# Transformer block on one core: the D weights of the up stage at another place in SBUF, and their passes in another order

## The chip, the core and the metric

The kernel runs on one core of a Trainium2 chip. The time is the device time of one execution in microseconds (us); three runs of the kernel before took 632.88, 635.07 and 636.14 us, so the median is 635.07 us. The core has five engines, each with an instruction stream of its own: TensorE (PE; its weight loads are listed apart, as PEld), VectorE (DVE), ScalarE (ACT), GpSimd (POOL) and SyncE (SP). Data lie in SBUF, in 128 partitions; an address here is a byte offset within a partition, the same for all partitions. TensorE sums into PSUM banks of 512 float32 per partition.

## The reference, cut to what matters

One transformer block over 512 tokens of width 1024. Around the change it is the feed-forward part:

```python
h = rmsnorm(x, mlp_pre_g)
gu = h @ w_gate_up                      # 1024 -> 2 * 2816
a, u = jnp.split(gu, [D_FF], axis=-1)
a = causal_dwconv(a, conv_w, conv_b)    # three taps along the tokens
y = (jax.nn.gelu(a, approximate=True) * u) @ w_down
x = x + rmsnorm(y, mlp_post_g)
```

Attention (compressed, selected, windowed) comes ahead of it, and a gated addition behind it. All in float32.

## The kernel before, in words

Every large product is done with split operands. A float32 matrix is cut into a high half (rounded to float32r, by ScalarE) and a low half (the rest, by VectorE: raw minus high). A product of weights w and activations x is then three passes of TensorE, w_high x_high + w_low x_high + w_high x_low, all summed into one PSUM tile. `mm3` (line 513) issues these three, in this order. One pass is one weight load of 128 x 128 and one matmul that streams 256 or 512 columns.

The up stage (`mlp_up`) makes the 22 pairs of 128 columns of "a" and "u". The first five pairs are done plainly. The other 17 ("blocked") use a scheme with seven half-size products in place of eight: `blocked_ops` (line 1743) writes, for each, the products named 1 to 7, each with four weight tiles of 128 x 128 times 256 columns, so 4 x 3 = 12 passes; 84 passes a block. Products 1 and 2 use the weights called A, 3 and 6 use X, 5 and 7 use Y, and product 4 uses D. X and its like are sums of loaded weights, made by VectorE. A, X and Y are 1024 wide and their halves live in two tiles each of tag "wh" (six tiles); D is 512 wide, and both its halves share one tile of tag "wd" (one tile, 1024 elements): high half in front, low half behind (`split_ops`, line 1639).

The activations of products 4, 5, 6 and 7 are sums of the normed input over token halves, made once by `half_ops` (line 1849) and split into tiles of 2 x 512 elements, high then low. Their tags are listed in `PTAG`. Product 4 uses the entries 1, 3, 5 and 7 of that list: one tile in "pt", one in "tt", one in "p", one in "kn".

The order of work: the up stage writes each operation with an engine, an estimated duration, its dependencies and a due time; `order` plays them through a small model, and the instructions are issued in the order that comes out. `products_in_order` fixes TensorE's own order: 2, 6, 7, 5, then product 1 of the next block, then 3 and 4. So product 4 is followed by product 2 of the next block. Product 4 is entered with a dependency on the low half of D. Each engine then runs its instructions strictly in that order, and waits at the first one whose input isn't there.

Where tiles lie: SBUF tiles of one pool are laid out by tag in the order in which the tags first appear, each tag taking the number of its tiles times the widest of them. The "u" tiles start at 5824, which is 192 modulo 512, and are 4096 bytes long, so all of them, with "pt" (from 182976) and "tt", are at 192 modulo 512. Tiles of "p" and "kn" are 1088 and 1216 elements wide (4352 and 4864 bytes, an odd multiple of 256), so they alternate between 192 and 448; the "kn" tile that product 4 reads is at 139200, which is 448. Behind "kn" stands a gap of 48 elements (192 bytes, `GAPS["wh"]`), which is made when the first "wh" tile is made (line 117, `real`), then the "wd" tile at 153984, then the six "wh" tiles from 158080. Both are at 384 modulo 512, so all weights of the up stage lie 192 bytes off the activations modulo 512, the low half of D too, since it starts 2048 bytes behind the high one.

Of the kernel before, what the change touches and what calls it, by code (L numbers as in the profile page):

```python
# [11 lines left out]
F32 = mybir.dt.float32  # L12
F32R = mybir.dt.float32r
# [4 lines left out]
P = 128  # L18
T = 512
D = 1024  # L20
# [21 lines left out]


SLOTS = {"u": 25, "kn": 4, "p": 6, "pt": 3, "tt": 2, "wh": 6, "wd": 1}
GAPS = {"wh": 48, "pt": 80}
P_WIDTH, KN_WIDTH = 1088, 1216


YTAG = ["u"] * 17 + ["kn"] * 3 + ["p"] * 2
# [38 lines left out]
PTAG = ["pt", "pt", "pt", "tt", "tt", "p", "p", "kn"]  # L88
# [16 lines left out]
class Tile:  # L105
# [11 lines left out]
    def real(self):  # L117
        if self.tile is None:
            pool, tag = self.rec.pools[self.pool], self.kw.get("tag")
            if self.pool == "up" and tag in self.rec.gaps:  # L120
                pool.tile([P, self.rec.gaps.pop(tag)], F32, tag="before_" + tag, name="before_" + tag, bufs=1)
                if tag == "wh":
                    pool.tile([P, D], F32R, tag="wd", name="wd", bufs=1)
            self.tile = pool.tile(list(self.shape), self.dtype, **self.kw)
        return self.tile

# [70 lines left out]
class Engine:  # L197
# [3 lines left out]
    def __getattr__(self, name):  # L201
        f = getattr(self.engine, name)
        if name == "to_reg":
            return f

        def call(*a, **k):
            if self.rec.on:
                return self.rec.add(self.name, name, a, k)
            return f(*map(real, a), **{m: real(x) for m, x in k.items()})  # L209

        return call
# [16 lines left out]
class Recorder:  # L228
    ENGINES = dict(tensor="PE", scalar="ACT", vector="DVE", gpsimd="POOL", sync="SP")

    def __init__(self, nc, pools):
        self.pools, self.nodes, self.on, self.over = pools, [], False, False
        self.strict, self.before = False, {}
        self.gaps = dict(GAPS)
        for e in self.ENGINES:
# [196 lines left out]
class Block:  # L432
# [1153 lines left out]
    def op(self, key, engine, us, run, deps=(), due=0.0, ready=0.0, takes=(), frees=()):  # L1586

        self.ops[key] = dict(engine=engine, us=us, run=run, deps=deps, due=due, ready=ready, takes=takes, frees=frees)
        return key
# [49 lines left out]
    def split_ops(self, key, src, n, due, deps, tag="wh", ready=-99.0, frees=(), low_deps=()):  # L1639

        nc, w = self.nc, self.w

        def high():
            if tag == "wh":
                w[key] = [self.up.tile([P, n], F32R, tag=tag, name=self.nm("wh"), bufs=SLOTS[tag]) for _ in range(2)]
            else:
                t = self.u([P, 2 * n], F32R, tag)
                w[key] = [t[:, i * n : (i + 1) * n] for i in range(2)]
            return [nc.scalar.activation(w[key][0], src(), AF.Copy)]

        def low():
            return [nc.vector.tensor_sub(w[key][1], src(), w[key][0].bitcast(F32))]

        if tag == "wh":
            deps, self.turn = deps + self.turn, ((key, "hi"),)
        self.op((key, "hi"), "ACT", HIGH_US if n == D else ACT_US, high, deps, due - 1.6, ready, takes=(tag,))
        self.op((key, "lo"), "DVE", LOW_US if n == D else TT_US, low, ((key, "hi"),) + low_deps, due, frees=frees)
# [85 lines left out]
    def blocked_ops(self, j, t, cyc):  # L1743

        nc, w = self.nc, self.w
# [3 lines left out]
        ht = self.ht  # L1749
        op = lambda i: (lambda k: ht[2 * k + i // 2][:, :, HALF[i % 2]])  # L1750
# [4 lines left out]
        n = BLOCKED.index(j)  # L1755
        fresh = n < len(ETAGS)
        etag = "ps" + ETAGS[n] if fresh else "e"
        tag = next(cyc)
# [35 lines left out]
        def product(ps, wt, first, op, begins=False, ends=False, wide=False):  # L1794
            def run():
                if wide and fresh:
                    self.banks.append(self.ps(ETAGS[n]))
                if ps == "h" and begins:
                    v["h"] = self.ps(tag)
                o = dict(h=lambda: v["h"][:, a], p=lambda: e()[:, a], q=lambda: e()[:, b])[ps]()  # L1800
                for k in range(4):
                    x = op(k)
                    if wide and fresh and k == 0:
                        hi, lo = (m[:, first * P : (first + 1) * P] for m in w[j, wt])
                        mm = functools.partial(nc.tensor.matmul, skip_group_check=True)
                        self.held(mm(e(), hi, x[:, None, 0, :].broadcast_to([P, 2, H]), start=True, stop=False))
                        mm(o, lo, x[:, 0, :], start=False, stop=False)
                        mm(o, hi, x[:, 1, :], start=False, stop=False)
                    else:
                        self.mm3(o, w[j, wt], (first + k) * P, x, begins and k == 0, ends and k == 3, keep=k == 0, shared=True)  # L1810
            return run
# [37 lines left out]
    def half_ops(self, due):  # L1849

        nc, fs, ht, ts = self.nc, self.f2, self.ht, []

        def sums(p, i):
            f = fs[p]
            b = lambda r, h: f[:, r, HALF[h]]
            if i == 0:
                ts.append(self.u([P, 4, H]))
            t = ts[p]
            if i == 0:
                q = f.rearrange("p r (h n) -> p (r h) n", h=2)  # L1860
                return [nc.vector.tensor_sub(t[:, 0:3:2, :], q[:, 0:4:3, :], b(0, 1)[:, None, :].broadcast_to([P, 2, H]))]
            if i == 1:
                return [nc.vector.scalar_tensor_tensor(t[:, 1, :], t[:, 0, :], -1.0, b(1, 1), op0=ALU.mult, op1=ALU.subtract)]
            return [nc.vector.scalar_tensor_tensor(t[:, 3, :], t[:, 1, :], -1.0, b(1, 0), op0=ALU.mult, op1=ALU.subtract)]

        part = lambda p, i: ts[p][:, 2 * i : 2 * i + 2, :].rearrange("p a n -> p (a n)")

        def high(p, i):
            ht.append(self.u([P, 2, T], F32R, PTAG[2 * p + i]))
            return [nc.scalar.activation(ht[2 * p + i][:, 0, :], part(p, i), AF.Copy)]  # L1870

        def low(p, i):
            o = ht[2 * p + i]
            return [nc.vector.tensor_sub(o[:, 1, :], part(p, i), o[:, 0, :].bitcast(F32))]

        prev = ()
        for p in range(KC // 2):
            t = due - 3.6 * (KC // 2 - 1 - p)
            for i in range(3):
                prev = self.op(("ht", p, i), "DVE", SUM_US if i else TT_US, functools.partial(sums, p, i), prev and (prev,), t - 3.5)  # L1880
            for i in range(2):
                prev = self.op(("ht", p, f"hi{i}"), "ACT", ACT_US, functools.partial(high, p, i), (prev,), t - 2)
                self.op(("ht", p, f"lo{i}"), "DVE", TT_US, functools.partial(low, p, i), (prev,), t)
# [286 lines left out]
```

## Time and profile before

| what | value |
|---|---|
| median of three runs | 635.07 us |
| profiled execution | 635.09 us, of which the span is 633.4 us |
| TensorE busy | 627.0 us (99% of the span), 4037 matmuls |
| VectorE busy | 513.4 us (81%) |
| ScalarE busy | 397.9 us (63%) |
| GpSimd busy | 156.5 us (25%) |
| up stage's blocked part | about 296 to 466 us of the span |

How to read it: the profile comes from one execution, so its rows are summed against 635.09 us. A row of a group names the line of the source (L209 is a helper's line that most of the second half of the kernel shares), the engine, the operation, the tile written and the tiles read (numbers left out), the shape and the count. "mlpup", "mlpdown", "norm" and "plegate" are stages, in this order; "psmm", "pss", "pst" and "pso" are PSUM tiles by their tag. A matmul of the up stage that reads "mlpup_u,mlpup_u" belongs to product 4, as D's weights are in a tile that is named like the activations. Durations of matmuls are modelled and overlap, so the time from one pass to the next is taken from their starts.

### The profile page before, as it was taken

What the parts mean: (1) busy time and instruction counts of PE and PEld (TensorE: products, weight loads), DVE (VectorE), ACT (ScalarE), POOL (GpSimd) and SP (SyncE); (2) the same over time, 40 slices, a digit from 0 to 9 for tenths busy, and PEclk for the clock granted to TensorE, in tenths of its full rate; (3) what the DMA queues carried; (4) which work ended last, traced back from release to release, by engine and by line L of the source; (5) the groups of instructions that cost most, each with busy time, mean ns of one, the idle gap of its engine ahead of it and who ended that gap; (6) DMA issues with size and microseconds to landing.
All of it is one profiled execution on the core that took longest, in us unless ns stands there. A gap on an engine that the chain in (4) does not pass through costs nothing.

```text
span 633.4 us, 11279 instructions
## 1 busy us (share of the span) xinstructions
PE 627.0 (99%) x4037; PEld 568.5 (90%) x4037; DVE 513.4 (81%) x1038; ACT 397.9 (63%) x773; POOL 156.5 (25%) x239
## 2 busy tenths in 40 slices
PE   9999999999999999999999999999999999999997
PEld 8988888888888887888999999999988999999986
DVE  6696679988967579699899999999998985856973
ACT  7546589889998568474676676766754543343251
POOL 2011397778686000211001100102100010201000
PEclk9999999999999999999999999999999999999999
DMA  8516922311321757485467576677844534367032
GB/s 296 172 76 213 230 79 67 84 45 40 77 74 52 283 203 294 161 206 116 121 197 182 169 164 182 162 209 212 218 129 126 156 95 122 116 252 266 2 116 84
DMA packets 45576, 95.79 MB, mean 151 GB/s; under 512 B 4560, under 2 KB 14160, under 8 KB 45264
## 3 DMA queue, kind: packets, MB, share of 16 engines
q1 hardware_dynamic: 40496, 84.57, 40.2%
q0 software_dynamic: 4880, 10.49, 9.9%
q8 instruction: 32, 0.52, 0.3%
q14 instruction: 24, 0.20, 0.1%
q10 hardware_dynamic: 144, 0.00, 0.0%
HBM read 81.42 MB, written 9.44 MB: 143 GB/s over the span
## 4 chain that ended last, share of the span: by engine, by line
PE 92%; DVE 6%; issue 1%; ACT 1%; ACTq 0%
PE mlpup_psmm L209 21%; PE fill_psmm L428 10%; PE mlpdown_pst L209 6%; PE mlpup_pss L209 6%; PE mlpdown_pss L209 5%; PE mlpdown_psmm L209 4%; PE nsa_pss L428 3%; DVE mlpup_u L209 3%; PE nsa_pso L428 3%; PE mlpup_pst L209 3%; PE norm_pss L209 3%; PE nsa_pst L428 3%; PE projq_psmm L428 3%; PE vnatural_pss L428 2%; PE projk_psmm L428 2%; PE compress_psmm L428 2%
## 5 line engine op out<-in xcount | busy, mean ns | idle before, releaser
L209 PE MATMUL mlpup_psmm<-r_u,mlpup_wh 128*128 128x256 f32 (+1 forms) x612 | 77.9, 280 | 0.0
L209 PEld LDWEIGHTS mlpup_psmm<-r_u,mlpup_wh 128*128 128x128 f32 x612 | 74.7, 188 | 0.3
L209 PE MATMUL mlpup_psmm<-mlpup_u,mlpup_wh 128*128 128x256 f32 (+1 forms) x474 | 69.1, 295 | 0.5 <-DVE mlpup_wh L209 0.5
L209 PEld LDWEIGHTS mlpup_psmm<-mlpup_u,mlpup_wh 128*128 128x128 f32 x474 | 62.6, 188 | 3.5 <-DVE mlpup_wh L209 0.9
L209 POOL DMA_DIRECT2D mlpup_u<-in_gs_dram x17 | 20.9, 1230 | 153.6 <-DVE mlpup_s L209 54.9
L209 ACT ACTIVATE mlpup_wh<-mlpup_u 128x1024 fp32r<-128x1024 f32 x37 | 39.2, 1061 | 17.6 <-PE mlpup_psmm L209 13.9
L209 ACT ACTIVATE mlpdown_wh<-mlpdown_wr 128x1024 fp32r<-128x1024 f32 (+1 forms) x24 | 23.7, 988 | 37.4 <-PE mlpdown_pst L209 8.8
L209 DVE TENSOR_TENSOR mlpup_wh<-mlpup_u,mlpup_wh 128x1024 fp32r<-128x1024 f32 x37 | 45.2, 1221 | 0.4 <-ACT mlpup_wh L209 0.3
L428 PE MATMUL fill_psmm<-loadx_u,fill_wh 128*128 128x512 f32 x144 | 45.0, 401 | 0.0
L209 PE MATMUL mlpdown_pst<-mlpup_u,mlpdown_wh 128*128 128x512 f32 (+1 forms) x228 | 44.6, 338 | 0.0
L209 PEld LDWEIGHTS mlpdown_pst<-mlpup_u,mlpdown_wh 128*128 128x128 f32 x228 | 36.8, 188 | 4.8
L428 POOL TENSOR_SCALAR nsa_u<-nsa_u,nsa_nrc,vnatural_u 128x512 f32<-128x512 f32 (+3 forms) x64 | 38.2, 610 | 8.3 <-DVE nsa_nrc L428 6.4
L209 DVE TENSOR_TENSOR mlpdown_wh<-mlpdown_wr,mlpdown_wh 128x1024 fp32r<-128x1024 f32 (+1 forms) x24 | 28.1, 1173 | 13.9 <-ACT mlpdown_wh L209 13.4
L209 DVE TENSOR_TENSOR mlpup_wh<-mlpup_wr,mlpup_wh 128x1024 fp32r<-128x1024 f32 (+1 forms) x23 | 27.9, 1212 | 11.3 <-ACT mlpup_wh L209 11.3
L428 ACT ACTIVATE nsa_u<-nsa_u,nsa_nnm 128x512 f32<-128x512 f32 (+3 forms) x64 | 35.3, 555 | 1.9 <-DVE nsa_nnm L428 1.6
L209 POOL TENSOR_TENSOR mlpdown_s<-mlpdown_s,mlpdown_s 128x512 f32<-128x512 f32 x6 | 10.0, 1664 | 104.7 <-ACT mlpdown_s L209 104.6
L209 PE MATMUL mlpdown_pss<-mlpup_u,mlpdown_wh 128*128 128x256 f32 x246 | 35.4, 279 | 0.0
L209 PEld LDWEIGHTS mlpdown_pss<-mlpup_u,mlpdown_wh 128*128 128x128 f32 x246 | 32.0, 188 | 0.3
L209 PE MATMUL mlpdown_psmm<-mlpup_u,mlpdown_wh 128*128 128x256 f32 (+1 forms) x180 | 30.9, 318 | 0.0
L428 DVE CUSTOM_DVE_ANT_0 nsa_u<-nsa_pss,vnatural_u 128x128 f32<-128x128 f32 (+4 forms) x64 | 27.4, 447 | 3.3 <-PE nsa_pss L428 1.9
L428 POOL TENSOR_TENSOR fill_wh<-fill_wr,fill_wh 128x1024 fp32r<-128x1024 f32 (+2 forms) x13 | 24.8, 1907 | 20.2 <-DMA compress_u<-projk_u 9.3
L209 ACT ACTIVATE mlpup_s<-mlpup_psmm 128x256 f32<-128x256 f32 x34 | 13.1, 384 | 26.4 <-PE mlpup_psmm L209 26.4
(346 smaller groups left out, 1667.1 us busy)
## 6 DMA issues: line engine op xcount, KB each, us to landing
mlpup_u<-in_gs_dram SPq DMA_DIRECT2D x34, 512.0 KB, 5.2
mlpup_u<-in_gs_dram POOLq DMA_DIRECT2D x17, 512.0 KB, 6.0
mlpup_wr<-in_gs_dram SPq DMA_DIRECT2D x17, 256.0 KB, 3.6
fill_wr<-in_win_dram SPq DMA_DIRECT2D x6, 512.0 KB, 4.0
fill_u<-fill_u SPq DMA_DIRECT2D x20, 128.0 KB, 2.3
mlpdown_wr<-in_down_dram SPq DMA_DIRECT2D x5, 512.0 KB, 3.8
compress_u<-projk_u SPq DMA_DIRECT2D x16, 128.0 KB, 3.4
kept_e<-pletiles_u SPq DMA_DIRECT2D x4, 512.0 KB, 5.2
```

The lines of the kernel that those rows point to most:

```text
L209: return f(*map(real, a), **{m: real(x) for m, x in k.items()})
L428: hold(x.call(*map(real, x.a), **{m: real(v) for m, v in x.k.items()}))
```

## The change

Three edits that belong together, and nothing else:

- The gap ahead of the weights goes, and the "wd" tile becomes 1072 elements wide in place of 1024, so that it starts 192 bytes earlier and ends where it did. The low half of D is put in front, at 153792, which is 192 modulo 512. The high half takes the last 512 elements, at 156032, which is 384 modulo 512 as before.
- The activation tile in "kn" is made 1216 elements wide (the width of its slot), and its 2 x 512 elements begin 64 elements (256 bytes) in, at 139456, which is 192 modulo 512.
- Product 4 no longer goes through `mm3`. Its 12 passes are the same, in a written order. In the list, k is the weight tile (0 to 3), q is 0 for the high and 1 for the low half of the weights, r is 0 for the high and 1 for the low half of the activations. The passes with the low half of the weights come at places 1, 6, 10 and 11 of the 12, where `mm3` had them at 2, 5, 8 and 11.

```diff
-GAPS = {"wh": 48, "pt": 80}
-P_WIDTH, KN_WIDTH = 1088, 1216
+GAPS = {"wh": 0, "pt": 80}
+P_WIDTH, KN_WIDTH, KN_SHIFT, WD_WIDTH = 1088, 1216, 64, 1072
...
             if self.pool == "up" and tag in self.rec.gaps:
-                pool.tile([P, self.rec.gaps.pop(tag)], F32, tag="before_" + tag, name="before_" + tag, bufs=1)
+                gap = self.rec.gaps.pop(tag)
                 if tag == "wh":
-                    pool.tile([P, D], F32R, tag="wd", name="wd", bufs=1)
+                    pool.tile([P, WD_WIDTH], F32R, tag="wd", name="wd", bufs=1)
+                else:
+                    pool.tile([P, gap], F32, tag="before_" + tag, name="before_" + tag, bufs=1)
...
-                t = self.u([P, 2 * n], F32R, tag)
-                w[key] = [t[:, i * n : (i + 1) * n] for i in range(2)]
+                t = self.u([P, WD_WIDTH], F32R, tag)
+                w[key] = [t[:, WD_WIDTH - n :], t[:, :n]]
...
+                if wt == "D":
+                    mm = functools.partial(nc.tensor.matmul, skip_group_check=True)
+                    order = ((0, 1, 0), (0, 0, 0), (0, 0, 1), (1, 0, 0), (1, 0, 1), (1, 1, 0),
+                             (2, 0, 0), (2, 0, 1), (3, 0, 0), (2, 1, 0), (3, 1, 0), (3, 0, 1))
+                    for i, (k, q, r) in enumerate(order):
+                        m = mm(o, w[j, wt][q][:, k * P : (k + 1) * P], op(k)[:, r, :], start=False, stop=i == 11)
+                        if i == 0:
+                            self.held(self.pin(m))
+                    self.last = m.ins
+                    return
...
-            ht.append(self.u([P, 2, T], F32R, PTAG[2 * p + i]))
+            if PTAG[2 * p + i] == "kn":
+                h = self.u([P, KN_WIDTH], F32R, "kn")[:, KN_SHIFT : KN_SHIFT + 2 * T].rearrange("p (s n) -> p s n", s=2)
+            else:
+                h = self.u([P, 2, T], F32R, PTAG[2 * p + i])
+            ht.append(h)
```

## The prediction

> **What bounds the kernel now.** I read the page first: busy shares, slices and the chain that ended last.
>
> ```profile
> span 633.4 us, 11279 instructions
> PE 627.0 (99%) x4037; PEld 568.5 (90%) x4037; DVE 513.4 (81%) x1038; ACT 397.9 (63%) x773; POOL 156.5 (25%) x239
> PEclk9999999999999999999999999999999999999999
> PE 92%; DVE 6%; issue 1%; ACT 1%; ACTq 0%
> ```
>
> TensorE is busy 99% and carries 92% of the chain, at full granted clock throughout. So only two things can shorten the span: fewer passes, or a shorter step from one pass to the next. The change keeps all passes. I therefore looked at the step, in the timeline of TensorE around the start of the blocked part of the up stage (columns: start, us, then the group; a group's length contains the drain of its last pass, so the step is taken from start to start).
>
> ```profile
> 297.20 1.54 PE L209 MATMUL mlpup_pss<-r_u,mlpup_wh 128*128 128x512 f32 x6
> 298.57 1.52 PE L209 MATMUL mlpup_psmm<-r_u,mlpup_wh 128*128 128x256 f32 x12
> 299.93 1.52 PE L209 MATMUL mlpup_psmm<-mlpup_u,mlpup_wh 128*128 128x256 f32 x12
> 301.29 0.28 PE L209 MATMUL mlpup_pss<-mlpup_u,mlpup_wh 128*128 128x256 f32 x1
> 301.99 1.57 PE L209 MATMUL mlpup_pss<-mlpup_u,mlpup_wh 128*128 128x256 f32 x11 [0.42 <-DVE mlpup_wh L209]
> 303.40 1.58 PE L209 MATMUL mlpup_psmm<-mlpup_u,mlpup_wh 128*128 128x256 f32 x12
> 304.81 3.10 PE L209 MATMUL mlpup_psmm<-r_u,mlpup_wh 128*128 128x512 f32 x24
> 307.75 1.57 PE L209 MATMUL mlpup_pss<-mlpup_u,mlpup_u 128*128 128x256 f32 x12
> 309.16 1.10 PE L209 MATMUL mlpup_psmm<-r_u,mlpup_wh 128*128 128x256 f32 x8
> ```
>
> From 298.57 to 301.29 two products of 12 passes take 2.72 us: **113.3 ns a pass**. Then TensorE waits once for a low half (the 0.42 us), and from there on a product of the same kind, on the same tiles, takes 1.41 us (303.40 to 304.81, 307.75 to 309.16): **117.8 ns a pass**. It never recovers: the last product of the blocked part starts at 464.63 and the next group at 466.04, again 1.41 us.
>
> ```profile
> 463.22 1.58 PE L209 MATMUL mlpup_pss<-mlpup_u,mlpup_u 128*128 128x256 f32 x12
> 464.63 1.58 PE L209 MATMUL mlpup_psmm<-r_u,mlpup_wh 128*128 128x256 f32 x12
> 466.04 5.90 PE L209 MATMUL mlpup_psmm<-mlpup_u,mlpup_wh 128*128 128x512 f32 x25
> 472.44 9.66 PE L209 MATMUL mlpup_psmm<-mlpup_u,mlpup_wh 128*128 128x512 f32 x41 [0.49 <-DVE mlpup_wh L209]
> ```
>
> So 256-column passes have two paces, which differ by 4.44 ns, and a stall can move the stream from the quick one to the slack one. Whole stages confirm it by the mean duration of a pass (second number behind the bar), which is 276 at the quick pace and 279 at the slack one:
>
> ```profile
> L209 PE MATMUL mlpdown_pss<-mlpup_u,mlpdown_wh 128*128 128x256 f32 x246 | 35.4, 279 | 0.0
> L209 PE MATMUL mlpdown_psmm<-mlpup_u,mlpdown_wh 128*128 128x256 f32 x120 | 17.0, 281 | 0.0
> L209 PE MATMUL mlpdown_pst<-mlpup_u,mlpdown_wh 128*128 128x256 f32 x108 | 16.8, 279 | 0.0
> L209 PE MATMUL norm_pss<-norm_u,mlpdown_wh 128*128 128x256 f32 x144 | 22.0, 284 | 0.0
> L209 PE MATMUL norm_psmm<-norm_u,mlpdown_wh 128*128 128x256 f32 x48 | 10.7, 277 | 0.0
> L209 PE MATMUL plegate_psmm<-norm_u,plegate_wh 128*128 128x256 f32 x24 | 2.9, 276 | 0.0
> ```
>
> The down stage runs at the slack pace, and the norm stage behind it has the clue. Three of its four products (norm_pss) take their weights from "u", "pt", "kn" and "tt" tiles, mostly at the activations' place modulo 512 bytes; the fourth (norm_psmm) takes them from "wh", 192 bytes off. The timeline there:
>
> ```profile
> 583.94 0.88 PE L209 MATMUL norm_pss<-norm_u,mlpdown_wh 128*128 128x256 f32 x6
> 584.66 0.39 PE L209 MATMUL norm_psmm<-norm_u,mlpdown_wh 128*128 128x256 f32 x2
> 584.88 0.52 PE L209 MATMUL norm_pss<-norm_u,mlpdown_wh 128*128 128x256 f32 x3
> ```
>
> Six passes with such weights take 0.72 us, 120 ns each: dearer themselves. But the two passes from "wh" behind them take 0.22 us, 110 to 115 ns by the rounding: the quick pace, though the down stage before ran at the slack one. So passes whose weights lie at the activations' place cost about 6.7 ns more than a quick one, and the stream comes out of them quick.
>
> The Trainium skill, "TensorE: Matmul & The Clock Gate", section "Step-by-step: what each phase is for", says that TensorE has two independent read ports, so that loading the next weights takes no read bandwidth from the running matmul. By it the place of the weights can't matter, and the time would stay at 635.1 us. This trace speaks against taking it whole: 120 and 113 ns alternate above with the tile that holds the weights.
>
> **The change part by part.** (1) *Place.* The D tile starts 192 bytes earlier, and its width of 1072 elements fills the old gap exactly, so the "wh" tiles stay where they are. Low halves move to 192 modulo 512, where the activations are; high halves stay at 384. The one activation tile of this product that lay elsewhere, in "kn" at 448, moves to 192 too. Instructions on ScalarE, VectorE and the queues keep their count, shape and order of issue: cost 0, and no DMA is touched.
>
> (2) *Order of the 12 passes, with the low half first.* The product is planned to wait for D's low half already, so no wait is added to the plan; in the machine the first pass now needs it, where the second did. Is it in time?
>
> ```profile
> 371.83 0.62 ACT L209 ACTIVATE mlpup_u<-mlpup_wr 128x512 fp32r<-128x512 f32 x1
> ...
> 365.85 1.23 DVE L209 TENSOR_TENSOR mlpup_wh<-mlpup_wr,mlpup_wh 128x1024 fp32r<-128x1024 f32 x1 [0.64 <-ACT mlpup_wh L209]
> 374.41 0.69 DVE L209 TENSOR_TENSOR mlpup_u<-mlpup_wr,mlpup_u 128x512 fp32r<-128x512 f32 x1
> 375.74 1.23 DVE L209 TENSOR_TENSOR mlpup_wh<-mlpup_wr,mlpup_wh 128x1024 fp32r<-128x1024 f32 x1 [0.64 <-ACT mlpup_wh L209]
> ...
> 377.00 1.22 PE L209 MATMUL mlpup_pso<-mlpup_u,mlpup_u 128*128 128x256 f32 x9
> ```
>
> The low half ends at 374.41 + 0.69 = 375.10, 1.90 us before the product at 377.00. Cost 0; if that cover went, all that follows on TensorE would wait, product 2 of the next block first.
>
> (3) *The pace behind the product.* No row shows passes alternating as they will here. Bounds: the stream stays slack (0), or every product of the blocked part from the first D product on is quick. That product runs at 307.75; between 309.16 and 466.04 lie 156.88 us, 111 products of 1.413 us. Of these 16 are D products and 95 are not. Quick, the 95 take 1.360 instead of 1.413: 95 x 0.0533 = **-5.07 us**. I take this end: the norm rows are the nearest, and there the stream turned quick within six passes; one D product has four such passes, and 17 of these products follow one another, so a turn that is missed at one can be caught at the next.
>
> (4) *The D products themselves.* Their four low passes at 120 and eight at 113.3 make 1.387 us, 0.027 less than now; with eight still slack it would be 1.422, 0.009 more. Over 16: -0.43 to +0.14. I take -0.2, between the two, as the passes right behind a low one need not be quick at once.
>
> (5) *What is late next.* Ahead of 472.44 TensorE waits 0.49 us for a low half of the down weights.
>
> ```profile
> 464.78 1.22 DVE L209 TENSOR_TENSOR mlpup_wh<-mlpup_wr,mlpup_wh 128x1024 fp32r<-128x1024 f32 x1 [0.57 <-ACT mlpup_wh L209]
> 471.17 1.22 DVE L209 TENSOR_TENSOR mlpup_wh<-mlpup_wr,mlpup_wh 128x1024 fp32r<-128x1024 f32 x1
> ```
>
> VectorE runs without a pause from 464.78 to that low half, and 464.78 itself hangs on TensorE's product that ended at 463.22. Two products lie between (463.22 and 464.63); about 0.1 us faster, they make this wait about 0.1 longer: **+0.1**.
>
> Does VectorE keep up before that? It works from 365.85 to 375.10, 9.25 us a block, and then idles 0.64 for a buffer that TensorE frees. A block of 84 passes takes 9.89 us now and would take 6 x 1.36 + 1.40 = 9.56. The idle shrinks to 0.31; TensorE stays the bound. In the stretches:
>
> ```profile
> 335.00:345.00 10.00, 10.00 (x87) 10.00 (x87) 9.50 (x13) 7.24 (x14) 1.22 (x1) 1.00 0.72 193
> 395.00:405.00 10.00, 10.00 (x87) 10.00 (x86) 9.21 (x12) 7.12 (x13) 1.21 (x1) 1.00 0.75 199
> ```
>
> VectorE's column (fourth) is 9.21 of 10 us in most blocks, 9.50 in the fullest; sped up by 3.4% that one is at 9.8, tight but no bound. DMA at 0.75 goes to 0.78 and stays hidden.
>
> **The sum.** -5.07 - 0.2 + 0.1 = -5.2 us. The profiled execution took 635.09 us (span 633.4 and 1.7 around it), 0.02 over the median of the runs, so 635.1 - 5.2 = **629.9 us**.
>
> **The rivals.**
> *Quick right through the down stage.* The quick pace can outlive 512-column passes: six of them lie between two quick stretches at 297.20. If the wait ahead of 472.44 went away or restarted the stream well, the 246 + 120 + 108 passes of the down stage would gain 4.44 ns each, 2.1 us: 627.8. Against it: the same wait, at the same pass, is followed by slack passes now, and I expect it a little longer.
> *Only part of the blocks.* Any new wait of TensorE makes the stream slack until the next D product, and VectorE's 9.50 is close. Half the gain: 632.5.
> *No turn.* The slack stream repeats itself product by product, so the D product always meets it alike; if its passes map slack to slack once, they do so 17 times. Then only term (4)'s bad end stays, 17 x 0.009 = 0.15: 635.2. For it: in norm_pss the six passes come in a row, here low passes stand mostly singly. Against it: the low ones at positions 10 and 11 are a pair, and four a block recur.
> *Slower.* The low passes leave the stream at a third pace, that of norm_pss, 120 ns a pass, until the next stall. From 309.16 on 1332 passes cost 2.2 ns more, 2.9 us; if it holds through the 474 of the down stage too, 1.0 more: 639.0. It decides once the wait ahead of 472.44 doesn't end it. Against it: the "wh" passes right behind norm_pss are at 113, not 120.
>
> **How the numbers follow.** Chances: the forecast 0.54, right through 0.08, part 0.11, no turn 0.20, slower 0.07. The forecast's own range is 628.2 to 631.6, as the three runs before spread by 1.6 us around their middle. About 0.5% (3.2 us) is what a measurement of this kernel can tell from no change, so faster means under 631.9. To it go nearly all of the forecast (0.51), right through (0.08) and a little of the part case (0.03): 0.62. The rest of these and no turn stay within: 0.31. Slower 0.07. For 8 in 10 the range takes in the part case and no turn and leaves out the slower one and the far end of right through: 627.8 to 635.9.
>
> **What would show it.** Right: from the first D product (near 307.7) on, products start 1.36 us apart, mean durations of mlpup_psmm fall from 279 to 276, a block takes 9.55 us, VectorE's idle per block falls to about 0.3 us, and the group now at 466.04 starts near 460.8. D's product at 1.39 us, or 1.41, tells term (4). Wrong: products still 1.41 us apart behind D; a wait ahead of D's first pass; or waits for VectorE scattered over the blocks, each with slack products behind it. If the down stage's passes drop to 276, the first rival holds.

## The result, and the profile after

The changed kernel took 630.33 us (median of ten runs, 629.89 to 633.30), the kernel before 633.73 us (ten runs, 632.51 to 636.45). The ratio is **0.9945, with a 95% interval of 0.9926 to 0.9963**: 0.55% faster, 3.4 us, a little over the 0.5% that can be told from no change. The forecast was 629.9 us, but its gain was 5.2 us from 635.1. So the time came out, and the gain did not; the profile shows why. The changed kernel's profiled execution took 630.13 us. Its page (span and busy shares):

```profile
span 628.4 us, 11280 instructions
PE 621.9 (99%) x4037; PEld 563.7 (90%) x4037; DVE 512.6 (82%) x1038; ACT 398.0 (63%) x773; POOL 157.0 (25%) x239
```

TensorE sets the end as before, with the same 4037 matmuls, in a span that is 5.0 us shorter. Where these 5.0 us lie is read off the starts in the timeline of TensorE. First the beginning of the blocked part in the changed kernel (start, us, group; "mlpup_u,mlpup_u" is product 4, called the D product from here on):

```profile
298.29 1.52 PE L211 MATMUL mlpup_psmm<-r_u,mlpup_wh 128*128 128x256 f32 x12
...
301.71 1.52 PE L211 MATMUL mlpup_pss<-mlpup_u,mlpup_wh 128*128 128x256 f32 x11 [0.43 <-DVE mlpup_wh L211]
303.07 1.52 PE L211 MATMUL mlpup_psmm<-mlpup_u,mlpup_wh 128*128 128x256 f32 x12
304.43 3.09 PE L211 MATMUL mlpup_psmm<-r_u,mlpup_wh 128*128 128x512 f32 x24
307.36 1.58 PE L211 MATMUL mlpup_pss<-mlpup_u,mlpup_u 128*128 128x256 f32 x12
308.78 1.52 PE L211 MATMUL mlpup_psmm<-r_u,mlpup_wh 128*128 128x256 f32 x12
310.14 1.52 PE L211 MATMUL mlpup_psmm<-mlpup_u,mlpup_wh 128*128 128x256 f32 x12
...
316.94 1.58 PE L211 MATMUL mlpup_pso<-mlpup_u,mlpup_u 128*128 128x256 f32 x12
318.36 1.57 PE L211 MATMUL mlpup_psmm<-r_u,mlpup_wh 128*128 128x256 f32 x12
319.77 1.57 PE L211 MATMUL mlpup_psmm<-mlpup_u,mlpup_wh 128*128 128x256 f32 x12
...
326.84 1.58 PE L211 MATMUL mlpup_pst<-mlpup_u,mlpup_u 128*128 128x256 f32 x12
328.26 1.52 PE L211 MATMUL mlpup_psmm<-r_u,mlpup_wh 128*128 128x256 f32 x12
```

Three D products are shown, at 307.36, 316.94 and 326.84. Behind the first, products start 1.36 us apart (308.78 to 310.14): the quick pace, 113.3 ns a pass, where the kernel before went on at 117.8. Behind the second they are 1.41 us apart again (318.36 to 319.77): slack. Behind the third they are quick. It goes on so to the end: **quick behind every odd D product of the 17, slack behind every even one**. The D product takes 1.42 us where it turns slack to quick (307.36 to 308.78, 326.84 to 328.26) and about as much, 1.42, where it turns quick to slack (316.94 to 318.36); from the starts in the trace the means are 1.420 and 1.415, and 1.413 before. The end of the blocked part, and the wait behind it:

```profile
463.10 5.88 PE L211 MATMUL mlpup_psmm<-mlpup_u,mlpup_wh 128*128 128x512 f32 x25
469.55 9.67 PE L211 MATMUL mlpup_psmm<-mlpup_u,mlpup_wh 128*128 128x512 f32 x41 [0.56 <-DVE mlpup_wh L211]
```

From the end of the first D product to the first 512-column group of the down weights there lie 463.10 - 308.78 = 154.32 us, and 156.88 before: **-2.56 us**. I call this stretch "the 111 products" below; its time is the measure of all experiments. By count: of the 95 products that are not D, 49 are quick (six behind each of eight D products, one behind the last) and gain 49 x 0.0533 = 2.61 us; the D products cost 8 x 0.002 + 8 x 0.007 = 0.07 more.

VectorE kept up. These are the two stretches of the prediction in the changed kernel (VectorE's column is the fourth time, after the length, PE and PEld), and then all of TensorE's waits for VectorE from 295 to 566 us (total, times, longest):

```profile
335.00:345.00 10.00, 10.00 (x87) 10.00 (x87) 9.04 (x12) 7.31 (x13) 1.22 (x1) 1.00 0.67 181
395.00:405.00 10.00, 10.00 (x88) 10.00 (x87) 9.33 (x13) 7.12 (x13) 1.21 (x1) 1.00 0.74 190
```

```profile
PE mlpup_psmm L211 <- DVE mlpup_wh L211: 0.6, 1, 0.6
PE mlpup_pss L211 <- DVE mlpup_wh L211: 0.4, 1, 0.4
```

No wait was added in the blocks. The two that are there are the two of the kernel before, 0.43 at 301.71 and 0.56 at 469.55.

The rest of the gain lies behind the up stage. The changed kernel's group in the down stage (count, busy us and mean ns of one behind the bar), and the start of the norm stage:

```profile
L211 PE MATMUL mlpdown_pss<-mlpup_u,mlpdown_wh 128*128 128x256 f32 x241 | 33.8, 276 | 0.0
```

```profile
578.97 0.88 PE L211 MATMUL norm_pss<-norm_u,mlpdown_wh 128*128 128x256 f32 x6
```

The mean is 276, which is quick; before it was 279, slack. From the group behind the wait to the norm stage: 578.97 - 469.55 = 109.42 us, and 583.94 - 472.44 = 111.50 before: **-2.08 us**. So the 5.0 us of the two profiled executions are -0.38 up to the end of the first D product (308.78 for 309.16), -2.56 in the 111 products, +0.05 around the wait, -2.08 in the down stage, and -0.03 behind it. Of the first, 0.28 is there at 298.57 already (298.29 after), ahead of anything that the change touches; the other 0.10 is the stretch behind the wait at 301.71, which came out quick in this execution as far as 304.43. The group there opens with a single 512-column pass, behind which the stream is slack. Whether the 2.08 belong to the change is the question that two of the experiments settle.

### The profile page after: what moved, and what is told of

Read it like the earlier page. It is cut to its first block, busy times and chain, and to the rows that moved or that the text cites. A ratio compares the mean times of both kernels' runs of the same rounds, so it can differ in the third digit from the quotient of the medians.

```text
span 628.4 us, 11280 instructions
## 1 busy us (share of the span) xinstructions
PE 621.9 (99%) x4037; PEld 563.7 (90%) x4037; DVE 512.6 (82%) x1038; ACT 398.0 (63%) x773; POOL 157.0 (25%) x239
## 4 chain that ended last, share of the span: by engine, by line
PE 92%; DVE 6%; issue 1%; ACT 1%; ACTq 0%
PE mlpup_psmm L211 21%; PE fill_psmm L430 10%; PE mlpdown_pst L211 6%; PE mlpup_pss L211 6%; PE mlpdown_pss L211 4%; PE mlpdown_psmm L211 4%; PE nsa_pss L430 3%; DVE mlpup_u L211 3%; PE nsa_pso L430 3%; PE mlpup_pst L211 3%; PE norm_pss L211 3%; PE nsa_pst L430 3%; PE projq_psmm L430 3%; PE vnatural_pss L430 2%; PE projk_psmm L430 2%; PE compress_psmm L430 2%
## 5 line engine op out<-in xcount | busy, mean ns | idle before, releaser
L211 PE MATMUL mlpup_psmm<-r_u,mlpup_wh 128*128 128x256 f32 (+1 forms) x612 | 76.5, 278 | 0.0
```

## The experiments

In each, the edit is given against the changed kernel. "The 111 products" is the stretch defined above: 156.88 us where all is slack, 154.32 in the changed kernel. The expectations speak of the theories as they stood when each was written; the theory at their start was that the D product moves the stream between the paces by the place of its low half, and its rivals were that the order does it wherever the weights lie, or that something with a period of two blocks does (a buffer, a PSUM bank).

**The place alone.** The low half lies in front as in the change, but the passes go in the order of `mm3`.

```diff
-                if wt == "D":
+                if wt == "D" and False:
```

> D's low halves and the kn tile at the new place, but the 12 passes of the D product in the old order (high, low, high for each weight tile). If the place alone turns the pace: products behind a D product start 1.36 us apart in at least half of the blocks, and the stretch from the end of the first D product to the first 512-column group of the down weights takes at most 154.4 us, as with the whole change (156.9 before it). If the order is needed too: 1.41 us apart in every block, stretch 156.9 to 157.3 us (four low passes dearer by 2 to 6 ns in 16 products).

Measured: 628.06 us in one execution. Its timeline of TensorE:

```profile
307.53 1.58 PE L211 MATMUL mlpup_pss<-mlpup_u,mlpup_u 128*128 128x256 f32 x12
308.94 1.52 PE L211 MATMUL mlpup_psmm<-r_u,mlpup_wh 128*128 128x256 f32 x12
...
317.10 1.58 PE L211 MATMUL mlpup_pso<-mlpup_u,mlpup_u 128*128 128x256 f32 x12
318.51 1.52 PE L211 MATMUL mlpup_psmm<-r_u,mlpup_wh 128*128 128x256 f32 x12
...
460.75 5.90 PE L211 MATMUL mlpup_psmm<-mlpup_u,mlpup_wh 128*128 128x512 f32 x25
```

The stream is slack ahead of the first D product (23 passes at 117.8 ns) and quick behind it, and it stays quick behind the second and all others: 460.75 - 308.94 = 151.81 us, 5.07 less than before, which is the whole of the prediction's term for the pace. The D product takes 1.41 us with a quick stream on both sides of it. So the place does it, and the new order, in this run, only gave half of it back.

**The order alone.** Both halves lie 192 bytes off the activations, as before the change, and the 12 passes go in the new order.

```diff
-                w[key] = [t[:, WD_WIDTH - n :], t[:, :n]]
+                w[key] = [t[:, WD_WIDTH - n :], t[:, WD_WIDTH - 2 * n : WD_WIDTH - n]]
```

> The new order of the 12 passes, kn tile moved, but D's low halves at 384 modulo 512 like the high ones. If the place is needed: every pass of the D product costs what the others cost, no product changes the pace, 1.41 us apart in all blocks, stretch 156.9 us. If the order alone does it: pace changes behind D products as with the whole change, stretch at most 154.4 us.

Measured: 634.85 us. From its timeline:

```profile
308.97 1.58 PE L211 MATMUL mlpup_psmm<-r_u,mlpup_wh 128*128 128x256 f32 x12
310.39 1.58 PE L211 MATMUL mlpup_psmm<-mlpup_u,mlpup_wh 128*128 128x256 f32 x12
...
465.85 5.90 PE L211 MATMUL mlpup_psmm<-mlpup_u,mlpup_wh 128*128 128x512 f32 x25
```

156.88 us, slack from end to end, as before. The order without the place does nothing in this run (which has the shifted "kn" tile too). Nor does a quick up stage come by chance without the place: with 635.09 - 5.07 = 630.0 us or less it would stand out, and none of the 40 timed runs of the kernel before on record, in this comparison and the later ones, lies under 632.5.

**The change in the first D product only.** `TURNED` names the blocks whose D product has the new place and order; the others have the old ones.

```diff
+TURNED = BLOCKED[:1]
...
-                w[key] = [t[:, WD_WIDTH - n :], t[:, :n]]
+                w[key] = [t[:, WD_WIDTH - n :], t[:, :n] if key[0] in TURNED else t[:, WD_WIDTH - 2 * n : WD_WIDTH - n]]
...
-                if wt == "D":
+                if wt == "D" and j in TURNED:
```

> New place and new order in the first blocked product's D alone; the other 16 have the old order and low halves at 384 modulo 512. Turn theory (a changed D product moves the stream by a fixed step and so swaps the two paces; passes 192 bytes off keep whichever they meet): the first D product turns the stream quick and nothing turns it back, 1.36 us a product through all blocks, stretch 156.9 - 111 x 0.0533 = 151.0 us, 3.3 us shorter than with the whole change. Bank theory (the pace follows the block's number, odd or even, as products 1, 2, 3, 5 and 6 change between two PSUM banks from block to block): quick in every other block, 154.3 us. Recovery theory (low passes at the activations' place pull the stream quick and it decays by itself within a block): quick in one block only, 156.5 us.

Measured: 635.99 us. From its timeline:

```profile
308.77 1.57 PE L212 MATMUL mlpup_psmm<-r_u,mlpup_wh 128*128 128x256 f32 x12
310.19 1.57 PE L212 MATMUL mlpup_psmm<-mlpup_u,mlpup_wh 128*128 128x256 f32 x12
...
463.94 1.68 PE L212 MATMUL mlpup_pss<-mlpup_u,mlpup_u 128*128 128x256 f32 x12 [0.95 <-ACT mlpup_pss L212]
```

Not as expected: the first D product, the same 12 passes as in the changed kernel, on a stream of the same mean pace, did not turn it. All 17 blocks are slack, and the 111 products took 158.10 us with a wait of 0.95 us for ScalarE at the last D product (463.94), which no other profile has. It comes from a late load: the weights issued at 455.75 landed at 462.38, 6.6 us later (2.9 in the kernel before, 456.14 to 459.07), and ScalarE had waited 1.89 us for them. What differs is seen in the step of each pass (ns from start to start, the 12 passes of one D product, from the records of matmuls):

```
changed kernel, from slack, leaves quick   117 116 122 117 118 123 118 116 119 120 121 113
changed kernel, from quick, leaves slack   121 118 117 119 115 118 118 117 117 118 115 122
here, from slack, leaves slack             119 117 118 118 115 118 118 117 117 118 115 122
```

The same passes meet the slack stream at another point here, and from the third pass on nearly run along the series that in the changed kernel ends slack. So the mean pace doesn't settle what a D product does. The theory of a fixed turn fell; in its place came this: the steps of a slack stream are a series, and where the stream ends depends on the point of the series at which the D product meets it. The steps fit that, but no run set the point by itself.

**The change in every other D product.**

```diff
+TURNED = BLOCKED[::2]
```

(with the two other lines of the experiment above)

> New place and new order in the D products of the blocks 1, 3, 5 and so on; old ones in the even blocks. Turn theory: the stream is quick for two blocks, slack for two blocks and so on: after D 1 quick, D 3 slack, D 5 quick; stretch about 154.3 us as with the whole change, in another pattern. Bank theory and a theory by which the changed D product always turns the stream quick: quick in all blocks, or quick in exactly every other one, never two and two.

Measured: 629.82 us. From its timeline, the first two D products (307.29 has the change, 316.87 doesn't), and the products behind the first, the second, the third (changed) and the fifth (changed):

```profile
307.29 1.58 PE L212 MATMUL mlpup_pss<-mlpup_u,mlpup_u 128*128 128x256 f32 x12
308.71 1.52 PE L212 MATMUL mlpup_psmm<-r_u,mlpup_wh 128*128 128x256 f32 x12
...
316.87 1.52 PE L212 MATMUL mlpup_pso<-mlpup_u,mlpup_u 128*128 128x256 f32 x12
318.23 1.52 PE L212 MATMUL mlpup_psmm<-r_u,mlpup_wh 128*128 128x256 f32 x12
...
327.81 1.57 PE L212 MATMUL mlpup_psmm<-r_u,mlpup_wh 128*128 128x256 f32 x12
...
347.60 1.52 PE L212 MATMUL mlpup_psmm<-r_u,mlpup_wh 128*128 128x256 f32 x12
```

The pattern is stretched from one block to two: quick behind the first changed D product and right through the unchanged one (316.87 to 318.23, 1.36 us), slack behind the next changed one (327.81) until the one after that (347.60). A period of two blocks given by buffers or banks would have stayed two blocks. So in this run each changed D product swaps the pace, in either direction, and one that isn't changed keeps it; the experiment before shows that the swap can be missed. The 111 products took 154.08 us.

**The place alone, timed.** The first experiment again, in several rounds on another chip.

> The new place with the old order again, timed against the kernel before. If a D product in the old order, with its low halves at the activations' place, leaves the stream quick from whatever pace it meets: all 17 blocks quick again, stretch 151.8 us, and a median 5 us or more below the kernel before when the down stage runs at the same pace in both (628 us). If the first look met a lucky pace: some blocks or all of them slack, stretch 154 to 157 us, median 630 to 635 us.

Measured: median 630.60 us of 12 runs, ratio 0.9958 (0.9934 to 0.9982). The profiled one took 628.07, all blocks quick, 151.81 us for the 111 products. But the runs fall in two heaps: 628.07 to 630.79 (seven) and 634.76 to 635.49 (five). Another execution, profiled later, fell in the other heap:

> A third look at the place alone in the old order, whose timed runs lie at 628 to 630.8 (7 of 12) and near 635 (5 of 12). If the runs near 635 are those in which the old order meets the slack stream at another point and leaves it slack: either a time near 635 with all blocks at 117.8 ns and a stretch of 156.9 us, or a time of 628 to 631 with all blocks quick and a stretch of 151.8 us; never a mixture of quick and slack blocks. If the D products act one by one on what they meet: a mixture.

```profile
308.49 1.58 PE L211 MATMUL mlpup_psmm<-r_u,mlpup_wh 128*128 128x256 f32 x12
309.90 1.57 PE L211 MATMUL mlpup_psmm<-mlpup_u,mlpup_wh 128*128 128x256 f32 x12
...
465.37 5.90 PE L211 MATMUL mlpup_psmm<-mlpup_u,mlpup_wh 128*128 128x512 f32 x25
```

634.35 us: slack behind the first D product (308.49 to 309.90) and to the end, 156.88 us. So with the place alone it is all or nothing. A quick stream stays quick, a slack one turns quick from some points only, and since in this order slack comes out as it went in, a turn that is missed at the first D product is missed at all 17. The changed kernel didn't miss it in either of its two profiles, and none of its ten timed runs lies above 633.30; but its 12 passes did miss it in the run with the first D product alone, and where it turns the stream quick it takes back half.

**Both halves at the activations' place.** The high half goes behind the low one, 2048 bytes on, so all 12 passes of the D product have their weights at 192 modulo 512, and the order is that of `mm3`.

```diff
-                w[key] = [t[:, WD_WIDTH - n :], t[:, :n]]
+                w[key] = [t[:, :n], t[:, n : 2 * n]]
...
-                if wt == "D":
+                if wt == "D" and False:
```

> Both halves of D at the activations' place modulo 512 bytes, old order: all 12 passes of the product like those of the norm stage whose weights lie there. Recovery theory (such passes pull the stream quick): D products 1.43 to 1.44 us (12 x 120 ns), all others 1.36, stretch 152.2 us. If only the alternation of the two places turns the pace: D 1.42 to 1.44 us and all others 1.41, stretch 157 us.

Measured: 628.04 us in one execution. From its timeline:

```profile
308.76 1.52 PE L211 MATMUL mlpup_psmm<-r_u,mlpup_wh 128*128 128x256 f32 x12
...
461.00 5.89 PE L211 MATMUL mlpup_psmm<-mlpup_u,mlpup_wh 128*128 128x512 f32 x25
```

152.24 us, quick behind all 17. Each later D product takes 1.440 us, 12 passes at 120 ns, the step that the norm stage shows for such passes: 0.027 dearer than the 1.413 of the place alone, which is the 0.43 us by which this stretch is longer than 151.81. Timed on another chip:

> Both halves of D at the activations' place, timed. Place-only runs lie at 628.1, 630.4 and 635, which the theory puts down to two independent things: the pace of the up stage (5 us) and of the down stage (2.3 us). If 12 passes in a row at the activations' place turn the stream quick from every pace, the up stage is quick in all runs: times near 628.0 and 630.4 only, none above 632, median 630.3 or less, ratio to the kernel before about 0.992. If this too depends on what it meets: some runs near 635 as with place only.

Median 630.40 us of six runs that lie from 630.21 to 630.70, ratio **0.9934 (0.9918 to 0.9951)**; none lies in a heap at 634. The profiled one again has 152.24 us and all blocks quick. What costs it 2.4 us beside the first execution is the down stage, which is slack here and was quick there:

```profile
L211 PE MATMUL mlpdown_pss<-mlpup_u,mlpdown_wh 128*128 128x256 f32 x239 | 34.6, 279 | 0.0
```

**The two kernels once more, unchanged.** Does the quick down stage belong to the change?

> The changed kernel once more, to see whether its pattern is fixed. Turn theory with a fixed entry: quick and slack blocks alternate again, stretch 154.3 us. If the down stage takes over the pace in which the up stage ends, it is quick again (508 passes at 113 to 114 ns) and the time is near 630.1; if that is settled anew at the wait ahead of the down weights, the time may also be near 632.5 with the down stage at 117.8 ns.

> The kernel before once more. Its ten runs lie near 632.7 and near 635.3. If the down stage's pace is what parts them: a time near 635 with the down stage at 117.8 ns, or near 632.7 with it at 113.3, in both cases with the blocked part at 117.8 and a stretch of 156.9 us. If it is the up stage that varies: a run near 632.7 has some quick blocks and a stretch near 154.5 us.

Measured: the changed kernel 632.25 us, the kernel before 632.93 us. The changed kernel, and then the kernel before:

```profile
L211 PE MATMUL mlpdown_pss<-mlpup_u,mlpdown_wh 128*128 128x256 f32 x224 | 32.8, 279 | 0.0
```

```profile
L209 PE MATMUL mlpdown_pss<-mlpup_u,mlpdown_wh 128*128 128x256 f32 x217 | 31.1, 276 | 0.0
```

The roles are swapped: the changed kernel's down stage is slack here, and that of the kernel before is quick. The 111 products took 154.32 and 156.88 us, as in the first profiles, and the changed kernel alternates as there. So the down stage falls on one pace or the other in both kernels, and that is worth 632.25 - 630.13 = 2.1 us in the changed one and 635.09 - 632.93 = 2.2 us in the one before. Like beside like the change gains 635.09 - 632.25 = 2.84 us with a slack down stage and 632.93 - 630.13 = 2.80 with a quick one. The runs of both kernels in the first comparison bear it out: the changed one has seven between 629.89 and 630.74 and three between 632.46 and 633.30. Of the ten runs of the kernel before, five lie between 632.51 and 633.17, and the median falls between the heaps; so medians of ten runs can differ by 3.4 us where like beside like differs by 2.8. Whether the change also makes a quick down stage likelier, ten runs each don't say. In the two later comparisons, each on another chip, only 3 of 28 runs of the kernel before lie under 633.2, and its medians are 634.98 and 634.81; so the share of quick down stages isn't fixed, and part of what the ratio says is that share.

What goes with the pace of the down stage can be read off single steps. The first 256-column passes there follow 90 passes of 512 columns. Soon behind the wait, the steps of these 90 repeat as 226, 229, 232 ns in all 14 profiles (mean 229). They end on the 232 (231 in two of them) in all seven whose down stage starts quick, and on one of the two other steps in the six that are slack throughout; the fourteenth is the last experiment below. So the pace seems to be settled by where the wait lets the stream into this cycle of three. That is a reading of 14 profiles; no run set it.

**Both halves at place for the first D product alone**, the others with both halves 192 bytes off, all in the order of `mm3`: does one turn last?

```diff
-                w[key] = [t[:, WD_WIDTH - n :], t[:, :n]]
+                w[key] = [t[:, :n], t[:, n : 2 * n]] if key[0] == BLOCKED[0] else [t[:, WD_WIDTH - n :], t[:, WD_WIDTH - 2 * n : WD_WIDTH - n]]
...
-                if wt == "D":
+                if wt == "D" and False:
```

> Both halves of D at the activations' place in the first blocked product alone; the other 16 have both halves 192 bytes off, all in the old order. If the pace is kept by all passes 192 bytes off until something turns it: first D 1.43 us, all 16 others 1.36, all blocks quick, stretch 111 x 1.36 = 151.0 us, 1.2 less than with both halves there in every block. If the quick pace has to be renewed: slack again within some blocks, 153 us or more.

Measured: 627.84 us. From its timeline:

```profile
308.94 1.52 PE L211 MATMUL mlpup_psmm<-r_u,mlpup_wh 128*128 128x256 f32 x12
...
449.46 1.68 PE L211 MATMUL mlpup_psmm<-r_u,mlpup_wh 128*128 128x256 f32 x12 [0.27 <-ACT mlpup_s L211]
...
460.87 5.90 PE L211 MATMUL mlpup_psmm<-mlpup_u,mlpup_wh 128*128 128x512 f32 x25
```

One turn lasts 140 us, through 14 D products that are themselves quick (1.36 us), until a wait of 0.27 us for ScalarE at 449.46; from there on the products are slack to the end. ScalarE had waited 2.67 us for a load of weights just before (issued at 439.37, landed at 448.12). 151.93 us for the 111 products is 0.12 over the place alone: the 14 quick D products save about 0.75, the wait costs 0.54 with its slow restart, and the slack passes behind it 0.32. A wait in one of the first blocks would have cost nearly all of the gain; that is an estimate from the 4.44 ns a pass, and no run shows it.

**The same reset ahead of the down stage.** With both halves at place in all D products, the first half-size weight of the down stage gets its high half into the D tile as well, so that the down stage's first 256-column passes have weights at the activations' place.

```diff
-                yield self.weight(a, 4 * n, early=True)
+                yield self.weight(a, 4 * n, early=True, tag=("wd", "wh") if c == g == 0 else "wh")
```

(beside the edits of "both halves at the activations' place")

> As the one with both halves at the activations' place, and the high half of the first weights of the down stage's half-size products is in the D tile too (192 modulo 512), its low half in wh as before: of the first 24 passes of 256 columns in the down stage 16 lie at the activations' place, at 120 ns for 113 or 118, 0.1 us in all. If such passes set the pace of what follows there too: down stage quick in all runs, all near 628.1, spread under 1 us, ratio about 0.990. If a low half 192 bytes off in between spoils it: times at 628 and 630.4 as without.

Measured: median **628.65 us of five runs, 628.31 to 629.10, ratio 0.9907 (0.9890 to 0.9924)**, the quickest of all that were timed, with no second heap. The down stage's group in its profile, and its timeline around a place where the pace was lost:

```profile
L211 PE MATMUL mlpdown_pss<-mlpup_u,mlpdown_wh 128*128 128x256 f32 x246 | 34.4, 276 | 0.0
```

```profile
451.52 1.60 PE L211 MATMUL mlpup_pst<-mlpup_u,mlpup_u 128*128 128x256 f32 x12
452.96 1.58 PE L211 MATMUL mlpup_psmm<-r_u,mlpup_wh 128*128 128x256 f32 x12
454.38 1.57 PE L211 MATMUL mlpup_psmm<-mlpup_u,mlpup_wh 128*128 128x256 f32 x12
...
458.61 1.59 PE L211 MATMUL mlpup_pss<-mlpup_u,mlpup_u 128*128 128x256 f32 x12
460.04 1.52 PE L211 MATMUL mlpup_psmm<-r_u,mlpup_wh 128*128 128x256 f32 x12
461.40 5.91 PE L211 MATMUL mlpup_psmm<-mlpup_u,mlpup_wh 128*128 128x512 f32 x25
```

The down stage's mean is the quick one, as meant, but not by the reset that was meant. Here are the steps (ns) of its first 42 passes of 256 columns, from 482.83 on, the 24 with the new place in them and the 18 behind; then the first steps of the 512-column passes that follow, and of the next 256-column passes, at 496.03:

```
24 passes  114 113 119 121 113 120 120 114 119 121 113 119 121 113 120 120 114 119 121 113 119 121 113 122
18 behind  118 117 118 118 117 119 117 118 118 118 117 118 118 117 119 117 118 118
512 col.   235 232 231 226 229 232 226 229 232 ...
256 col.   113 113 114 113 113 114 ...
```

The 18 passes behind the new ones are slack, 117.8 ns. The stream is quick only from the 512-column passes on: after three odd steps their cycle of three is the one that the quick down stages have. The 90 passes ahead of all this ended on 226, as in three of the six slack down stages (226, 226 and 225). So the edit did change what follows, but by way of another point in the cycle and not by leaving the stream quick; that it does so in every execution is read from the five times alone, as one was profiled.

In the up stage a single pass at 450.09 has a step of 134 ns, about 20 ns late, without any wait that the profile shows, and the passes behind it are slack. It is the first pass of the product at which the experiment before had its wait, and ScalarE had again waited for a late load (2.15 us, landed at 448.66); a wait too short to be listed is likely, but not shown. The D product at 451.52 meets the slack passes and doesn't turn them (452.96 to 454.38 is 1.42); the last one, at 458.61, does. So twelve passes at the place turn the stream mostly, not always: in all profiles such a D product met a slack stream six times, and left it quick five times.

## Why the prediction was right, and by which steps

The time of the likeliest case was 629.9 us, the profiled one 630.1 and the median 630.3. That is luck, two errors that cancel in the sum: the pace behind the D products gave 2.5 us less than forecast (-2.6 for -5.07), and the down stage, left where it was in the forecast, gave 2.1 us in that profile. Against the median of ten runs before, 633.73, the gain is 3.4 us for a forecast of 5.2.

- **What bounds the kernel**: right. All the gain is in the step from pass to pass, at the same count of passes and under a full clock.
- **(1) The place, cost 0 on other engines**: right. VectorE 512.6 and ScalarE 398.0 us for 513.4 and 397.9.
- **(2) The low half first, cost 0**: right. No wait stands ahead of any D product's first pass.
- **(3) The pace behind the product, -5.07**: this is the step that failed. Measured: -2.6, half. That such passes move the stream from the slack pace to the quick one was right, and that the quick pace lasts through a block too. Wrong was the half-sentence that "a turn that is missed at one can be caught at the next", which counts only turns to quick: the product turns a quick stream slack as well. The bounds (0 to -5.07) held it. I had read the norm rows, six passes in a row, as saying that passes at the place leave the stream quick; the runs show it for 12 in a row (five times in six), and not for four among 12. Two passes at about 113 ns behind such ones were too little to read a quick stream from: in the last experiment's down stage single passes step at 113 among the dear ones, and the stream behind them is slack.
- **(4) The D products, -0.2**: +0.07, inside the bounds (-0.43 to +0.14), near the end where the passes behind a low one stay dear. The row for eight passes at 113.3 was the wrong one to average in: the list of steps above has 116 and more for all but one or two of the twelve.
- **(5) The wait ahead of the down weights, +0.1**: 0.49 to 0.56, +0.07, right. The two products ahead of it got about 0.05 us faster (1.42 and 1.36 us for twice 1.413), where 0.1 was taken.
- **VectorE as the next bound**: did not happen, as forecast (9.04 and 9.33 of 10 us). What came late in the quickest up stages was another thing, loads of D's weights: two profiles with a quick stream lost it close to 450 us, where ScalarE had waited over 2 us for one.
- **The rivals.** "Only part of the blocks" (632.5) had the size of what the up stage did, and the wrong mechanism: no wait was added, the D product undoes its own turn. With a slack down stage the changed kernel takes 632.25, close to that rival's time. "Quick right through the down stage" took place in the profiled execution; the wait did restart the stream well, which was one of its conditions. The repeat with a slack down stage shows that the change doesn't ensure it. "No turn" is what the place alone does in one of its three profiles and, by their times, in five of its 12 timed runs, and the profile fits its reason: the slack stream meets each of the 17 D products nearly alike, and none turns it. I had tied that to the wrong kernel. "Slower", a third pace of 120 ns that lasts, did not happen: 120 ns are the passes at the place themselves, and those behind them step at 113.3 or 117.8.
- **The forecast's base.** The profiled execution before had a slack down stage (635.09); ten runs put the median at 633.73. I took one execution's down stage as the kernel's own, and the down stage's pace as settled by the wait ahead of it, since "the same wait, at the same pass, is followed by slack passes now". The repeat of the kernel before has that wait and quick passes behind it.
- **The rule of the Trainium skill** weighed there ("TensorE: Matmul & The Clock Gate", section "Step-by-step: what each phase is for"), by which TensorE's two read ports are independent: what the prediction drew from it, that the place of the weights can't matter, the runs contradict. The order alone left everything slack, the place alone made all 17 blocks quick in two of three profiles, and with a quick stream the same 12 passes take 1.44 us with all weights at the activations' place and 1.36 us with all of them 192 bytes off.

## What to carry to other kernels

Where passes of one shape have two steps in the trace, look for what turns one into the other before counting instructions: here 4.4 ns a pass, on 95 x 12 passes of the blocks and 474 of the down stage, 7.2 us in all. An edit that moves such a state has to be judged from both entries, slack and quick, and the profile of one execution shows only one of the histories, so take two profiles of the kernel before as well. Where a cheap state is kept once it is reached, a few dearer passes can pay for themselves: both halves of D at the activations' place, with one such tile at the head of the down stage, took 628.65 us, against 630.33 for the change, though each of those passes is dearer itself. The two medians come from different comparisons (the kernel before had 634.81 in one and 633.73 in the other), and the second half of that edit worked otherwise than meant.

## What the hardware showed that I had not expected

- TensorE's stream of 256-column passes with weights 192 bytes off the activations modulo 512 has two paces, 113.3 and 117.8 ns, and keeps either for as long as nothing disturbs it: slack for over 1300 passes in the kernel before, quick for over 1100 where one D product had turned it.
- Little is needed to lose the quick pace: a wait of 0.27 us, or one step that was 20 ns late. But a wait doesn't always lose it: behind 0.43 us at 301.71 the stream was quick in the changed kernel (301.71, then 303.07 to 304.43: 1.36) and slack in the one before. In the two profiles of 14 in which it was quick there, it came out slack behind the one 512-column pass that follows; groups of 18, 24, 36 and 42 such passes in the down stage left a quick stream quick.
- Passes with weights at the activations' place cost 120 ns in a row of their own and mostly leave the stream quick. The slack pace is at least two states with one mean, told apart only by the steps of single passes: from a slack stream the later 512-column groups of the down stage begin with steps of about 234 and 236 ns in three profiles, and of about 230 and 231 in three others.
- The down stage's pace, which differs from execution to execution of one kernel, is worth 2.1 to 2.2 us, and with it most of the spread of the kernel before, whose runs lie in heaps 2 to 3 us apart.
- Open: which accesses clash, and why 512 bytes; what sets the point at which a D product meets the slack stream; and what the shift of the "kn" tile does alone, which wasn't tried (with the new order and the old place, it left the stream slack). That reads of weights and activations collide by their address is argued from the place alone, not shown.
